# A fused two-layer encoder on one core: normalization moved to ScalarE, page sums made in place, and the starts of three stages rearranged

## The chip, the cores and the metric

The kernel runs on one core of a Trainium2 chip. TensorE (PE) multiplies matrices into eight PSUM banks, VectorE (DVE) and ScalarE (ACT) work on tiles in SBUF and read those banks, GpSimd (POOL) and SyncE (SP) here do little more than start transfers between SBUF and DRAM. Each engine takes its instructions in a fixed order: an instruction that waits holds up all that stand behind it on its engine. The metric is the time of one execution in microseconds (us), lower is better.

## The reference, cut to what matters

An encoder trunk of two layers on x of 1024 positions by 1024 columns, in float32. Layer 0 mixes with attention and a Fourier transform, layer 1 with a spatial gating unit; after each mixer stands a SwiGLU feed-forward network (FFN).

```python
def odd_mixer(x, w_in, norm_g, norm_b, w_s, b_s, w_out):
    z = jax.nn.gelu(x @ w_in, approximate=False)
    u, v = jnp.split(z, 2, axis=-1)                # 2048 columns each
    v = layer_norm(v, norm_g, norm_b)
    vc = v.reshape(B, S // 128, 128, 8, 256)       # chunks, positions, 8 head groups, columns
    s = jnp.einsum('gpq,bnqgc->bnpgc', w_s, vc) + jnp.swapaxes(b_s, 0, 1)[None, None, :, :, None]
    return (u * s.reshape(B, S, 2048)) @ w_out

def swiglu(x, w_gate, w_up, w_down):               # 2816 columns
    return (jax.nn.silu(x @ w_gate) * (x @ w_up)) @ w_down

# each layer
x = layer_norm(DN_ALPHA * x + mixer(x), ...)
x = layer_norm(DN_ALPHA * x + swiglu(x, ...), ...)
```

## The kernel before

**Products.** Every large product is a Strassen-Winograd scheme on a 2 by 2 split: seven products of sums in place of eight. The left operands are sums of the quarters of x (`A11`, `A12`, `A22`, `S1` to `S4`), held transposed for the whole stage; the right operands are sums of the quarters of the weight cells (`t1` to `t4`, `b11`, `b21`, `b22`). A float32 operand is split into a high part, rounded by a cast on ScalarE (L135), and a low part, what is left, by a subtraction on VectorE (L136); `mm3` (L141 to L143) makes high by high, low by high and high by low. One of the seven products of a unit is 12 matmuls of 512 columns. The names tell the side: `xah`/`xal` and `xoh`/`xol` are the halves of left operands, `whi`/`wlo` those of weights, `raw` are loaded weights, `rx` loaded pages, `b` PSUM banks.

**FFN.** `ffn` goes over 22 units of columns. A unit's weights come from `right_operands` (L587), which makes four pairs of tiles `whi`/`wlo`, t4 and t1 in the second of its casts. Those of the first two units are made while the stage before still runs. `seven` (L610) is a generator; each `go(u, 1)` issues one product. The late half of x comes out of the layer norm just before: `turn0` (L490) turns a tile of 128 positions through PSUM by 8 transposes on TensorE, scales and shifts it by 8 instructions on ScalarE (`turned`, L357 to L365), and splits it into `A11` and `A12`; `all_sums` then makes `S2` to `S4`. The first products of units 0 and 1 (t4, t1, on the half that is already there) are issued between the four turns. `v_pair` (L845) does the same at the start of the odd layer, with the columns of v.

**Spatial loop.** After v (written to DRAM as `vd`), a loop over the 8 head groups g (L818) makes u: unit g is seven products, and among them stand four jobs `mixed(n)` of the group before. A job loads its 512 columns of v (`load`), takes mean and deviation off them in four instructions on VectorE (`normed`, L799, for the next job), multiplies them by the position matrix `w_s` into a bank (L808, 8 matmuls of 128 columns), adds the biases (L809, VectorE), and multiplies the page of u in place (L811). `emit` (L823) combines the banks into the page on VectorE (L825) and applies Gelu on ScalarE (L826). A finished page is stored (`tp`, held as `st["H"]`); every two pages `direct` (L343) makes their sums (`page_sums`, L316 to L319, VectorE) into two fresh `raw` tiles and stores them as `SA` and `SB`. The loads of the coming weights use the same four `raw` buffers.

**Output product.** `reduce` loads stored pages, sums and the sums of the output weights (`TA`, `TB`) and multiplies them. The last four jobs (28 to 31) of the loop run among its first products.

A tile's buffer is reused in turn, and who takes it waits for its last reader. `issue_after` and `behind` hold an instruction's place in the order behind another one; a scheduler settles the rest of the order of each engine from the code.

## Time and profile before

| | |
|---|---|
| median of 3 runs | 2571.9 us (2570.29 to 2572.54) |
| profiled execution | 2572.24 us, of which the span from the first to the last instruction is 2570.4 us |
| TensorE busy | 2471.8 us |
| VectorE, ScalarE, GpSimd busy | 1840.0, 1073.5, 308.4 us |
| mean granted clock of TensorE | 0.981 |

The span is what the trace shows; some 2 us of each execution lie around it. The granted clock is the share of TensorE's full speed (2.4 GHz) that it was given, and its two levels are 1.0 and 0.5. A busy TensorE at half clock counts as busy, so the two have to be read together.

### The profile page before, as it was taken

The page shows a single profiled execution, that of the slowest core. Times are in us where ns is not written, and L with a number is a line of the kernel's source. Part 1 is how long each engine was busy: PE and PEld are TensorE (multiplying, and loading weights), DVE is VectorE, ACT ScalarE, POOL GpSimd, SP SyncE. Part 2 cuts the span into 40 slices and gives each one's busy share as a digit, 9 for nine tenths or more (in the row PEclk, how much of TensorE's full clock was granted, in tenths as well). Part 3 has the DMA queues.
Part 4 walks back from the last instruction along what each step waited for, and adds up shares of the span by engine and source line. Part 5 has one row for each costly group of instructions (what it writes and reads, how often), then busy time and mean ns, then how long its engine had stood idle before and what let it go on. Part 6 is the DMA issues. An engine that isn't in the chain of part 4 may idle for free. (4 is left out here: it accounts for less than half of the span.)

```text
span 2570.4 us, 33123 instructions
## 1 busy us (share of the span) xinstructions
PE 2471.8 (96%) x12294; PEld 2083.3 (81%) x12294; DVE 1840.0 (72%) x2673; ACT 1073.5 (42%) x1643; POOL 308.4 (12%) x511
## 2 busy tenths in 40 slices
PE   8989999999999999999999999898999999999997
PEld 6778888887778888878889997776878888887886
DVE  4448878757886667668677767788788766766757
ACT  3335545544653333334355442232474333333332
POOL 1000111010110111110011223221010101101001
PEclk9999999999999999999999999899999999999999
DMA  4122433147334454486645644457634544549554
GB/s 173 42 88 70 143 110 112 62 162 265 127 139 139 173 188 150 161 300 233 205 164 189 214 160 148 147 205 270 228 121 148 175 153 165 188 143 332 198 187 147
DMA packets 164073, 431.95 MB, mean 168 GB/s; under 512 B 19880, under 2 KB 26696, under 8 KB 163912
## 3 DMA queue, kind: packets, MB, share of 16 engines
q1 hardware_dynamic: 108216, 232.11, 27.5%
q0 software_dynamic: 55696, 197.73, 20.6%
q8 instruction: 96, 1.57, 0.3%
q14 instruction: 65, 0.53, 0.1%
HBM read 286.64 MB, written 138.41 MB: 165 GB/s over the span
## 5 line engine op out<-in xcount | busy, mean ns | idle before, releaser
L141 PE MATMUL b<-xoh,whi 128*128 128x512 f32 x1040 | 411.5, 396 | 20.3 <-ACT whi L135 18.4
L136 DVE TENSOR_TENSOR wlo<-raw,whi 128x1024 fp32r<-128x1024 f32 (+3 forms) x277 | 302.7, 1099 | 173.5 <-ACT whi L135 171.0
L135 ACT CAST whi<-raw 128x1024 fp32r<-128x1024 f32 (+3 forms) x277 | 260.6, 953 | 385.3 <-PE b L142 223.6
L135 ACT CAST xoh<-rx 128x1024 fp32r<-128x1024 f32 (+1 forms) x252 | 244.3, 1011 | 421.1 <-PE b L142 323.4
L143 PE MATMUL b<-xoh,wlo 128*128 128x512 f32 x1040 | 408.2, 393 | 0.3
L142 PE MATMUL b<-xol,whi 128*128 128x512 f32 x1040 | 408.3, 393 | 0.0
L136 DVE TENSOR_TENSOR xol<-rx,xoh 128x1024 fp32r<-128x1024 f32 (+1 forms) x252 | 287.3, 1168 | 166.1 <-ACT xoh L135 165.6
L142 PE MATMUL b<-xol,xoh 128*128 128x512 f32 x960 | 380.0, 396 | 17.7 <-DVE xol L136 17.7
L141 PE MATMUL b<-xoh 128*128 128x512 f32 x960 | 377.9, 396 | 14.5 <-ACT xoh L135 14.5
L143 PE MATMUL b<-xoh,xol 128*128 128x512 f32 x960 | 376.9, 393 | 0.0
L141 PEld LDWEIGHTS b<-xoh,whi 128*128 128x128 f32 x1040 | 197.7, 190 | 62.5 <-ACT whi L135 19.4
L143 PEld LDWEIGHTS b<-xoh,wlo 128*128 128x128 f32 x1040 | 197.1, 190 | 44.0 <-DVE wlo L136 3.1
L142 PEld LDWEIGHTS b<-xol,xoh 128*128 128x128 f32 x960 | 183.4, 191 | 59.1 <-DVE xol L136 21.0
L142 PEld LDWEIGHTS b<-xol,whi 128*128 128x128 f32 x1040 | 197.7, 190 | 41.0 <-issue 0.2
L141 PEld LDWEIGHTS b<-xoh 128*128 128x128 f32 x960 | 183.9, 192 | 54.2 <-ACT xoh L135 15.8
L143 PEld LDWEIGHTS b<-xoh,xol 128*128 128x128 f32 x960 | 183.0, 191 | 38.1
L624 ACT COPY y<-b 128x512 f32<-128x512 f32 x200 | 116.6, 587 | 214.2 <-PE b L143 210.1
L141 PE MATMUL b<-xah,whi 128*128 128x512 f32 x416 | 164.9, 396 | 0.1
L142 PE MATMUL b<-xal,whi 128*128 128x512 f32 x416 | 164.0, 394 | 0.0
L143 PE MATMUL b<-xah,wlo 128*128 128x512 f32 x416 | 162.4, 391 | 0.0
L131 DVE TENSOR_TENSOR raw<-raw,raw 128x512 f32<-128x512 f32 (+1 forms) x172 | 127.2, 739 | 24.0 <-DMA raw<-w_up 18.8
L669 DVE TENSOR_TENSOR y<-b,y 128x512 f32<-128x512 f32 x84 | 58.0, 690 | 81.4 <-PE b L143 81.4
(377 smaller groups left out, 4582.8 us busy)
## 6 DMA issues: line engine op xcount, KB each, us to landing
raw<-w_gate SPq DMA_DIRECT2D x44, 512.0 KB, 3.6
raw<-w_up SPq DMA_DIRECT2D x44, 512.0 KB
q<-w_down POOLq DMA_DIRECT2D x44, 512.0 KB, 5.2
h<-x POOLq DMA_DIRECT2D x44, 512.0 KB, 3.8
rx<-h SPq DMA_DIRECT2D x60, 256.0 KB, 3.1
rx<-w_down SPq DMA_DIRECT2D x60, 256.0 KB, 4.9
raw<-o_v SPq DMA_DIRECT2D x16, 512.0 KB, 5.2
x<-o_out POOLq DMA_DIRECT2D x16, 512.0 KB, 6.2
```

Source lines behind the costliest of these rows:

```text
L131: self.nc.vector.tensor_tensor(out, a, b, op=ALU.subtract)
L135: a = self.nc.scalar.copy(hi, src)
L136: return a.ins, self.nc.vector.tensor_tensor(lo, src, hi.bitcast(F32), op=ALU.subtract).ins
L141: mm(ps, lh, rh, start=start, stop=False, skip_group_check=skip)
L142: mm(ps, lh, rl, start=False, stop=False, skip_group_check=skip)
L143: mm(ps, ll, rh, start=False, stop=stop, skip_group_check=skip)
L624: nc.scalar.copy(t, ps)
L669: self.last_v = nc.vector.tensor_tensor(sb, ps, sb, op=op).ins
```

## The change

1. **Second unit of the FFN.** `early_operands`, a generator, takes the place of `right_operands` for unit 1 of each FFN. Its first step makes only t4 and t1, into the first free pair of tiles, ahead of the stage; the second step (b11 with b21, t2 with t3, b22) is taken after `sums`.
2. **Late tiles by twos.** `turned_two` turns two tiles together: the 16 transposes write banks of 2 by 256 columns, and 8 instructions of 256 columns on ScalarE take the place of 16 of 128. The splits take 1024 columns. The same for v (`pend` in `v_pair`).
3. **Normalization on ScalarE.** `normed` is an ACTIVATE with scale 1/deviation and bias `shift` = -mean/deviation, and is placed behind the last Gelu (`last_a`).
4. **Page sums in place.** The sums of the pages of group g are made by `summed(g)` in the pages themselves, two units later (after product 0 of unit g+2), and stored from there; no `raw` tiles are taken.
5. **Pages stored by halves.** Each job stores its 512 columns: 32 stores of 256 KB in place of 16 of 512 KB.
6. **End of the loop.** Job 28 moves into unit 7; jobs 29 to 31 and the sums of groups 6 and 7 run in the output product.

```diff
-                    w0[l].append(self.right_operands(*gate_up(l)(1)))
+                    rest = self.early_operands(*gate_up(l)(1))
+                    w0[l].append((next(rest), rest))
+    def turned_two(self, zs, tiles, gT, bT):
+        ws = [t.rearrange("p (k c) -> p k c", k=4) for t in tiles]
+        pss = [self.bank(i, (P, 2, 256)) for i in range(4)]
+        for k in range(8):
+            for i, z in enumerate(zs):
+                nc.tensor.transpose(pss[k // 2][:, k % 2, i * P:(i + 1) * P], z[:, k * P:(k + 1) * P], self.ident)
+        for k in range(8):
+            nc.scalar.activation(ws[k // 4][:, k % 4, :], pss[k // 2][:, k % 2, :], AF.Identity, bias=bT[:, k:k + 1], scale=gT[:, k:k + 1])
+    def early_operands(self, w1, w2):
+        self.sub(v[:, hi], u[:, lo], g[:, lo])
+        self.sub(v[:, lo], u[:, hi], v[:, hi])
+        self.sub(v[:, lo], v[:, lo], g[:, hi])
+        cells(v, "t4", "t1")
+        yield out
+        cells(g, "b11", "b21")
+        self.sub(v[:, lo], u[:, hi], v[:, hi])
+        self.sub(v[:, hi], u[:, hi], u[:, lo])
+        cells(v, "t2", "t3")
+        cells(u[:, hi], "b22")
...
-                with self.tc.issue_after(self.last_v):
+                with self.tc.issue_after(self.last_a):
-                        nc.vector.tensor_scalar(vz, vz, mv[:, t, 0:1], rstd[:, t:t + 1], op0=ALU.subtract, op1=ALU.mult)
+                        nc.scalar.activation(vz, vz, AF.Identity, bias=shift[:, t:t + 1], scale=rstd[:, t:t + 1])
...
-                if half == 1:
-                    nc.gpsimd.dma_start(st["H"][j], pg[j])
-                    if jj == 1:
-                        self.direct(st, g, pg.pop(j - 1), pg.pop(j), self.raw_tile)
+                nc.gpsimd.dma_start(st["H"][j][:, c], pg[j][:, c])
+            def summed(g, *marks):
+                with self.behind(*marks):
+                    self.page_sums(p0, p1, p0, p1)
+                nc.gpsimd.dma_start(st["SA"][g], p0)
+                nc.gpsimd.dma_start(st["SB"][g], p1)
...
+                    if g > 1 and i == 0:
+                        summed(g - 2, self.last_v)
+                    if g == 7 and i == 6:
+                        mixed(28)
-            return [lambda n=n: mixed(n) for n in range(28, 32)]
+            return [lambda: mixed(29), lambda: (summed(6, self.marks[2]), mixed(30)), lambda: mixed(31), lambda: summed(7, self.marks[2])]
```

**How the order moves.** First, ScalarE at the start of the first FFN. Before: `raw997` to `raw999` are unit 1's weights; whi1002 is its b11 and b21, whi1000 its t4 and t1, and `q1089` is the third late tile.

```order
L135 CAST whi1002_5996<-raw997_5989 128x1024
L365 ACTIVATE q1089_6687<-b1090_6688,bT951_5615,gT950_5614 128x128
L624 COPY y1085_6662<-b1084_6649 128x512
L365 ACTIVATE q1089_6687<-b1090_6688,bT951_5615,gT950_5614 128x128 x3
L365 ACTIVATE q1089_6687<-b1091_6689,bT951_5615,gT950_5614 128x128 x4
L135 CAST xah1079_6624<-q1089_6687 128x4x128
L135 CAST whi1000_5994<-raw999_5993 128x1024
L135 CAST xah1079_6624<-q1089_6687 128x4x128
L624 COPY y1085_6662<-b1092_6710 128x512
L365 ACTIVATE q1093_6724<-b1094_6725,bT951_5615,gT950_5614 128x128 x4
```

Now, at the same place (`q1084` is the first half of the third and fourth tile together; whi1093 is unit 1's b11 and b21):

```order
L135 CAST xah1073_6611<-x1075_6613 128x1024
L135 CAST xah1073_6611<-x1076_6614 128x1024
L135 CAST whi1093_6775<-raw997_5989 128x1024
L378 ACTIVATE q1084_6676<-b1086_6678,bT951_5615,gT950_5614 128x256 x2
L378 ACTIVATE q1084_6676<-b1087_6679,bT951_5615,gT950_5614 128x256
L663 COPY y1082_6660<-b1081_6647 128x512
L663 COPY y1082_6660<-b1083_6662 128x512
L378 ACTIVATE q1084_6676<-b1087_6679,bT951_5615,gT950_5614 128x256
L378 ACTIVATE q1085_6677<-b1088_6680,bT951_5615,gT950_5614 128x256 x2
L378 ACTIVATE q1085_6677<-b1089_6681,bT951_5615,gT950_5614 128x256 x2
L135 CAST xah1073_6611<-q1084_6676 128x1024
```

The cast of t4 and t1 is gone from between the late tiles. It stands some 40 rows further up ScalarE's order, among the casts of the pages `rx` of the product before:

```order
L135 CAST xoh_5606<-rx1010_6101 128x1024
L135 CAST xoh_5606<-rx1011_6106 128x1024
L135 CAST whi1000_5997<-raw999_5993 128x1024
L135 CAST xoh_5606<-rx1012_6135 128x1024
L135 CAST xoh_5606<-rx1013_6140 128x1024
```

Second, VectorE in the spatial loop, at the border of two units. Before, with the sums of the finished pages x1864 and x1865 between a job and the next `normed`:

```order
L799 TENSOR_SCALAR whi1828_13322<-whi1828_13322,vmv1824_13316,vrs1825_13317 128x128 x4
L809 SCALAR_TENSOR_TENSOR wlo1829_13323<-b1900_13838,og1826_13318,q1831_13325 128x512
L811 TENSOR_TENSOR x1865_13516<-x1865_13516,wlo1829_13323 128x512
L316 TENSOR_TENSOR raw1902_13849<-x1864_13515,x1865_13516 128x512
L317 TENSOR_TENSOR raw1901_13848<-x1864_13515 128x512
L318 TENSOR_TENSOR raw1901_13848<-raw1902_13849,x1864_13515 128x512
L825 TENSOR_TENSOR x1889_13706<-b1896_13764,y1892_13721 128x512
L319 TENSOR_TENSOR raw1902_13849<-x1865_13516,raw1901_13848 128x512
L825 TENSOR_TENSOR x1890_13707<-b1896_13764,y1892_13721 128x512
L799 TENSOR_SCALAR whi1828_13322<-whi1828_13322,vmv1824_13316,vrs1825_13317 128x128 x4
L809 SCALAR_TENSOR_TENSOR whi1828_13322<-b1918_13918,og1826_13318,q1831_13325 128x512
```

Now, at the same border some units later (line numbers are shifted: L317 to L320 are the sums, L849 and L851 a job's biases and its product with the page):

```order
L136 TENSOR_TENSOR wlo1957_14228<-raw1947_14216,whi1956_14227 128x512
L317 TENSOR_TENSOR x1911_13848<-x1910_13847,x1911_13848 128x512
L849 SCALAR_TENSOR_TENSOR whi1828_13276<-b1962_14262,og1826_13271,q1831_13279 128x512
L318 TENSOR_TENSOR x1910_13847<-x1910_13847 128x512
L851 TENSOR_TENSOR x1933_14038<-x1933_14038,whi1828_13276 128x512
L319 TENSOR_TENSOR x1910_13847<-x1911_13848,x1910_13847 128x512
L131 TENSOR_TENSOR raw1972_14411<-raw1971_14409,raw1970_14407 128x512
L320 TENSOR_TENSOR x1911_13848<-x1911_13848,x1910_13847 128x512
L849 SCALAR_TENSOR_TENSOR whi1828_13276<-b1964_14296,og1826_13271,q1831_13279 128x512
L136 TENSOR_TENSOR wlo1976_14415<-raw1970_14407,whi1975_14414 128x1024
L851 TENSOR_TENSOR x1933_14038<-x1933_14038,whi1828_13276 128x512
```

The `normed` rows are gone from VectorE, and the sums are those of the group before the last, written into the pages x1910 and x1911 themselves. On ScalarE the `normed` rows (L839) now stand behind Gelu (L872), with casts of weights and copies of banks between them:

```order
L872 ACTIVATE x1865_13472<-x1865_13472 128x512
L839 ACTIVATE whi1828_13276<-whi1828_13276,vshift_13273,vrs1825_13270 128x128 x4
L135 CAST whi1885_13642<-raw1876_13631 128x512
L872 ACTIVATE x1864_13471<-x1864_13471 128x512
L872 ACTIVATE x1865_13472<-x1865_13472 128x512
L839 ACTIVATE whi1828_13276<-whi1828_13276,vshift_13273,vrs1825_13270 128x128 x2
L663 COPY y1890_13671<-b1889_13658 128x512
L839 ACTIVATE whi1828_13276<-whi1828_13276,vshift_13273,vrs1825_13270 128x128 x2
L839 ACTIVATE wlo1829_13277<-wlo1829_13277,vshift_13273,vrs1825_13270 128x128 x4
L135 CAST whi1904_13829<-raw1899_13822 128x1024
```

Third, VectorE at the end of the loop, where the output product's first page operands (`xol` from `rx`) are made. Before:

```order
L136 TENSOR_TENSOR xol_5607<-rx2053_14921,xoh_5606 128x1024
L136 TENSOR_TENSOR xol_5607<-rx2054_14926,xoh_5606 128x1024
L825 TENSOR_TENSOR x2017_14674<-b2021_14703,y2025_14757 128x512
L799 TENSOR_SCALAR whi1828_13322<-whi1828_13322,vmv1824_13316,vrs1825_13317 128x128 x4
L809 SCALAR_TENSOR_TENSOR wlo1829_13323<-b2033_14819,og1826_13318,q1831_13325 128x512
L136 TENSOR_TENSOR xol_5607<-rx2055_14931,xoh_5606 128x1024
L811 TENSOR_TENSOR x1992_14483<-x1992_14483,wlo1829_13323 128x512
L825 TENSOR_TENSOR x2016_14673<-b2023_14731,y2019_14688 128x512
L316 TENSOR_TENSOR raw2035_14830<-x1991_14482,x1992_14483 128x512
L317 TENSOR_TENSOR raw2034_14829<-x1991_14482 128x512
L318 TENSOR_TENSOR raw2034_14829<-raw2035_14830,x1991_14482 128x512
L825 TENSOR_TENSOR x2017_14674<-b2023_14731,y2019_14688 128x512
```

Now (`gb` rows, L469 and L470, are the residual of the layer norm; x2005 is the last page, whose sums begin in the last row):

```order
L320 TENSOR_TENSOR x1982_14433<-x1982_14433,x1981_14432 128x512
L851 TENSOR_TENSOR x2005_14624<-x2005_14624,wlo1829_13277 128x512
L136 TENSOR_TENSOR xol_5607<-rx2047_14984,xoh_5606 128x1024
L849 SCALAR_TENSOR_TENSOR wlo1829_13277<-b2046_14930,og1826_13271,q1831_13279 128x512
L136 TENSOR_TENSOR xol_5607<-rx2048_14989,xoh_5606 128x1024
L851 TENSOR_TENSOR x2005_14624<-x2005_14624,wlo1829_13277 128x512
L469 TENSOR_TENSOR y2033_14831<-y2033_14831,gb2044_14910 128x1024
L136 TENSOR_TENSOR xol_5607<-rx2049_15026,xoh_5606 128x1024
L469 TENSOR_TENSOR q2031_14829<-q2031_14829,gb2044_14910 128x1024
L470 TENSOR_TENSOR y2033_14831<-y2033_14831,gb2045_14912 128x1024
L317 TENSOR_TENSOR x2005_14624<-x2004_14623,x2005_14624 128x512
```

and, five rows later, the end of those sums, four additions of finished banks (L457), and the next page operand:

```order
L320 TENSOR_TENSOR x2005_14624<-x2005_14624,x2004_14623 128x512
L457 SCALAR_TENSOR_TENSOR x2030_14828<-x2030_14828,b2034_14832 128x512
L457 SCALAR_TENSOR_TENSOR q2031_14829<-q2031_14829,b2035_14839 128x512
L457 SCALAR_TENSOR_TENSOR q2032_14830<-q2032_14830,b2037_14858 128x512
L457 SCALAR_TENSOR_TENSOR y2033_14831<-y2033_14831,b2038_14865 128x512
L136 TENSOR_TENSOR xol_5607<-rx2050_15031,xoh_5606 128x1024
```

Before, the sums went into `raw` tiles and stood behind no store; now the sums of the last two groups are in VectorE's order between the operands of the output product, and the operand from rx2050 stands behind them.

## Rows read from the trace of the kernel before

**Rows 1.** Page, part 1, TensorE: busy time, share of the span, instructions.

```profile
PE 2471.8 (96%) x12294; PEld 2083.3 (81%) x12294; DVE 1840.0 (72%) x2673; ACT 1073.5 (42%) x1643; POOL 308.4 (12%) x511
```

**Rows 2.** The waits of TensorE over the whole span: in total, times, longest.

```profile
PE b L141 <- ACT whi L135: 18.4, 5, 6.0
...
PE b L141 <- ACT xoh L135: 14.5, 3, 7.0
PE b L808 <- issue: 7.7, 3, 2.8
```

**Rows 3.** Windows: length, each engine's busy time, granted clock, DMA share, GB/s.

```profile
690.00:742.00 52.00, 46.00 (x208) 37.28 (x208) 44.28 (x71) 36.90 (x73) 6.91 (x11) 0.93 0.25 86
1905.00:1960.00 55.00, 48.19 (x219) 38.97 (x218) 48.36 (x76) 39.11 (x76) 6.27 (x10) 0.97 0.29 101
1360.00:1405.00 45.00, 40.57 (x309) 39.72 (x309) 40.64 (x67) 26.38 (x44) 11.23 (x21) 0.92 0.61 211
1550.00:1715.00 165.00, 147.37 (x692) 121.98 (x691) 125.23 (x245) 46.61 (x68) 45.93 (x70) 0.93 0.43 152
1715.00:1790.00 75.00, 64.81 (x279) 52.71 (x279) 65.69 (x88) 24.93 (x30) 12.96 (x22) 0.91 0.84 289
```

**Rows 4.** Timeline of TensorE, first FFN start: start, length, idle before, releaser.

```profile
707.12 0.80 PE L141 MATMUL b<-xoh,whi 128*128 128x512 f32 x1 [5.00 <-ACT whi L135]
...
727.13 0.50 PE L141 MATMUL b<-xoh,whi 128*128 128x512 f32 x1 [0.97 <-ACT q L624]
```

**Rows 5.** Timeline of ScalarE at the same place.

```profile
697.76 2.59 ACT L365 ACTIVATE x<-b,bT,gT 128x128 f32<-128x128 f32 x7
...
701.18 1.14 ACT L135 CAST whi<-raw 128x1024 fp32r<-128x1024 f32 x1
...
705.87 1.20 ACT L135 CAST whi<-raw 128x1024 fp32r<-128x1024 f32 x1
```

**Rows 6.** Timeline of VectorE at the same place.

```profile
704.35 1.42 DVE L131 TENSOR_TENSOR raw<-raw,raw 128x512 f32<-128x512 f32 x2
```

**Rows 7.** Timeline of VectorE and then TensorE, start of the odd layer's v.

```profile
1363.18 1.29 DVE L136 TENSOR_TENSOR xal<-q,xah 128x512 fp32r<-128x512 f32 x2 [3.51 <-ACT xah L135]
...
1393.74 0.35 PE L862 MATMUL b<-whi,xah 128*128 128x256 f32 x1 [2.15 <-DVE y L873]
```

**Rows 8.** Timeline of TensorE, spatial loop: a product between two stretches, a wait.

```profile
1645.71 0.39 PE L141 MATMUL b<-xah,whi 128*128 128x512 f32 x1
...
1648.43 1.05 PE L808 MATMUL b<-q,whi 128*128 128x128 f32 x8
...
1591.80 0.46 PE L808 MATMUL b<-q,whi 128*128 128x128 f32 x2 [2.76 <-issue]
```

**Rows 9.** Timeline of VectorE ahead of that wait.

```profile
1587.74 0.69 DVE L316 TENSOR_TENSOR raw<-x,x 128x512 f32<-128x512 f32 x1
...
1591.36 0.85 DVE L799 TENSOR_SCALAR whi<-whi,vmv,vrs 128x128 f32<-128x128 f32 x3
```

**Rows 10.** Groups by line and form in 1550 to 1715 us, VectorE and ScalarE.

```profile
L799 DVE TENSOR_SCALAR wlo<-wlo,vmv,vrs 128x128 f32<-128x128 f32 x48 | 14.8, 349 | 0.0
L799 DVE TENSOR_SCALAR whi<-whi,vmv,vrs 128x128 f32<-128x128 f32 x48 | 13.3, 343 | 0.0
...
L809 DVE SCALAR_TENSOR_TENSOR wlo<-b,og,q 128x512 f32<-128x512 f32 x13 | 9.7, 747 | 0.0
...
L826 ACT ACTIVATE x<-x 128x512 f32<-128x512 f32 x24 | 15.2, 632 | 51.1 <-DVE x L825 51.1
```

**Rows 11.** DMA issues in 1550 to 1715 us, then 1715 to 1790 us.

```profile
tp<-x POOLq DMA_DIRECT2D x12, 512.0 KB, 3.5
...
oddSA<-raw POOLq DMA_DIRECT2D x6, 512.0 KB, 4.1
...
tp<-x POOLq DMA_DIRECT2D x4, 512.0 KB, 8.3
```

**Rows 12.** Timeline of ScalarE at the start of the odd layer's output product.

```profile
1756.92 2.95 ACT L135 CAST xoh<-rx 128x1024 fp32r<-128x1024 f32 x3 [10.41 <-DMA rx<-tp]
```

More of the change, by code (lines that the diff above doesn't have):

```diff
@@ L366, in turned @@
         return w[:, 0:4, :], w[:, 4:8, :]
+    def turned_two(self, zs, tiles, gT, bT):
+        nc = self.nc
+        ws = [t.rearrange("p (k c) -> p k c", k=4) for t in tiles]
[5 more added lines that the diff above has]
+            nc.scalar.activation(ws[k // 4][:, k % 4, :], pss[k // 2][:, k % 2, :], AF.Identity, bias=bT[:, k:k + 1], scale=gT[:, k:k + 1])
+        return ws
     def source(self, st, p, m):
@@ L488, in turn1, with turn0 @@
             kept[1, s] = l, h
-        def turn0(s):
-            l, h = self.turned(xt[0, s], (0, 1) if s % 2 == 0 else (2, 3), self.m_tile("xxqq"[s]), gT, bT)
-            self.split(*self.operand(self.A11, s), l)
-            self.late = self.split(*self.operand(self.A12, s), h)[1]
-            kept[0, s] = l, h
+        def turn0(q):
+            ws = self.turned_two([xt[0, 2 * q + i] for i in range(2)], [self.m_tile("xq"[q]) for _ in range(2)], gT, bT)
+            for o, w in zip((self.A11, self.A12), ws):
+                self.late = self.split(*(x[:, q] for x in self.left(o)), w)[1]
+            for i in range(2):
+                kept[0, 2 * q + i] = tuple(w[:, :, i * P:(i + 1) * P] for w in ws)
         def sums(s):
@@ L579, in all_sums @@
                     sums(s)
-        return [lambda s=s: turn0(s) for s in slots], all_sums
+        return [lambda q=q: turn0(q) for q in range(2)], all_sums
     def bcast(self, t, src):
@@ L608, in right_operands, with cells @@
         return out
+    def early_operands(self, w1, w2):
+        g, u = self.raw(w1), self.raw(w2)
+        v = self.raw_tile()
+        lo, hi = self.LO, self.HI
+        out = {}
+        def cells(src, *names):
+            h, l = self.wpair()
+            w = 512 * len(names)
+            self.split(h[:, :w], l[:, :w], src)
+            for i, n in enumerate(names):
+                out[n] = tuple(x[:, i * 512:(i + 1) * 512].rearrange("p (k c) -> p k c", k=4) for x in (h, l))
+        self.sub(v[:, hi], u[:, lo], g[:, lo])
[8 more added lines that the diff above has]
+        cells(u[:, hi], "b22")
+        yield
     def seven(self, w, banks, tiles, emit):
@@ L687, in ffn @@
         w0, w1 = w0
-        u0 = unit(0, w0, "yq")
+        w1, rest = w1
+        u0, u1 = unit(0, w0, "yq"), unit(1, w1, "yq")
         turns[0]()
-        self.go(u0, 1)
+        self.go(u0, 2)
         turns[1]()
-        turns[2]()
-        self.go(u0, 1)
-        turns[3]()
-        u1 = unit(1, w1, "yq")
         self.go(u1, 2)
         sums()
+        next(rest)
         self.go(u0, 5)
@@ L755, in spatial @@
             mv, rstd, ogT, obT = (self.m_tile(n, s, 1) for n, s in (("vmv", (P, NT, 2)), ("vrs", (P, NT)), ("og", (P, 16)), ("ob", (P, 16))))
+            shift = self.small.tile([P, NT], F32, tag="ms", name="vshift")
             for t, n in ((ogT, "o_gT"), (obT, "o_bT")):
@@ L766, in stats @@
                 self.rstd_of(rstd, mv[:, :, 1], LN_EPS)
+                nc.vector.tensor_tensor(shift, mv[:, :, 0], rstd, op=ALU.mult)
+                nc.vector.tensor_scalar(shift, shift, -1.0, None, op0=ALU.mult)
             def biases(i):
@@ L812, in mixed @@
                 load(n + 4)
-                if half == 1:
-                    nc.gpsimd.dma_start(st["H"][j], pg[j])
-                    if jj == 1:
-                        self.direct(st, g, pg.pop(j - 1), pg.pop(j), self.raw_tile)
+                c = slice(half * 512, (half + 1) * 512)
+                nc.gpsimd.dma_start(st["H"][j][:, c], pg[j][:, c])
+            def summed(g, *marks):
+                p0, p1 = pg.pop(2 * g), pg.pop(2 * g + 1)
+                with self.behind(*marks):
+                    self.page_sums(p0, p1, p0, p1)
+                nc.gpsimd.dma_start(st["SA"][g], p0)
+                nc.gpsimd.dma_start(st["SB"][g], p1)
             for g in range(8):
@@ L825, in emit @@
                     self.last_v = nc.vector.tensor_tensor(u, ps, sb, op=op).ins
-                    nc.scalar.activation(u, u, AF.Gelu)
+                    self.last_a = nc.scalar.activation(u, u, AF.Gelu).ins
                 unit = self.seven(w, [(4, 5, 6, 7, 0, 1)[(g * 4 + i) % 6] for i in range(4)], "yy", emit)
@@ L886, in v_pair @@
             for b in range(2):
-                if pend is not None and (n, b) in ((4, 0), (4, 1), (5, 0), (5, 1)):
-                    pend[0][(n - 4) * 2 + b]()
+                if pend is not None and b == 0 and n in (4, 5):
+                    pend[0][n - 4]()
                 if n == 4:
```

## The prediction

> **What bounds the kernel now.** The page comes first: TensorE is busy for 2471.8 of 2570.4 us [rows 1], so the time is its matmuls, the gaps between them, and what it loses at half clock. The view of its waits says who ends the gaps: weights that ScalarE has yet to cast (18.4 us in five waits), page operands that it has yet to cast (14.5 in three), and jobs of the spatial loop (7.7 in three) [rows 2]. Third, the windows of the five stages that the change touches [rows 3]. I read each as: loss = (length - TensorE busy) + (1 - granted clock) x length, the second term for matmuls that took longer at half clock (it counts idle time at half clock too, so it errs upward).
>
> - FFN of layer 0, 690 to 742: 6.0 + 3.6 = 9.6 us.
> - FFN of layer 1, 1905 to 1960: 6.8 + 1.7 = 8.5.
> - Start of v, 1360 to 1405: 4.4 + 3.6 = 8.0.
> - Spatial loop, 1550 to 1715: 17.6 + 11.6 = 29.2.
> - Output product, 1715 to 1790: 10.2 + 6.7 = 16.9.
>
> Together 72 us: no edit here removes a matmul of a product, so that is the most that the change can give. In none of the five is VectorE or ScalarE busy throughout [rows 3]. What counts is where they are late.
>
> **FFN starts.** TensorE sits idle for 5.00 us until the cast of unit 1's weights [rows 4]. ScalarE casts one pair at 701.18, VectorE then makes two more differences at 704.35, and only at 705.87 comes the cast of t4 and t1 [rows 5, 6]. The change makes this pair in the stage before, where its cast and differences (some 1 us and 3 x 0.7 us) stand beside the output product's own work. So the wait goes. What is late next are the sums S2 to S4: the last wait of this start, 0.97 us at 727.13, is for them and what stands around them [rows 4]. They need all four turns. A turn's 8 instructions take 2.59/7 = 0.37 us each [rows 5], 32 of them 11.8 us. An instruction of 256 columns is not in the trace; below it lies 0.37, above it 0.63 (an ACTIVATE of 512 [rows 10]); nearer the lower end I take 0.44, so 16 x 0.44 = 7.0 us, 4.8 saved on ScalarE. That brings the sums some 4 us forward, while TensorE, without its wait, would be there some 8 us earlier: it waits again, about 3 us plus the half clock behind it. Of 9.6 us lost some 6 stay: **3.5 us gained**, bounds 0 and 7. The second FFN has the same waits in the same order (loss 8.5): **3.5 us**, the same bounds.
>
> **Start of v.** VectorE waits 3.51 us for ScalarE's casts of the last turn [rows 7] and then works nearly without a break; some 30 us later TensorE waits for that backlog, 2.15 us at the longest [rows 7]. Turning by twos saves the same 4.8 us on ScalarE, of which some 3 reach the first sum, since transposes and products stand between. A backlog that starts 3 us earlier takes most of 4.4 us of idle time and part of the clock's 3.6: **4.5 us**, bounds 0 and 7.
>
> **Spatial loop.** A product takes 1648.43 - 1645.71 = 2.72 us [rows 8], so a unit of seven with four jobs (8 matmuls of a quarter width, an estimate of 0.45 us) 20.8 us; the window holds (165 - 29.2)/20.8 = 6.5 units, and loses 4.5 us in each. The row that shows how: the page sums begin at 1587.74 on VectorE, `normed` stands behind them and comes only at 1591.36 [rows 9], and TensorE's job waits 2.76 us for it [rows 8]. The longest wait, 6.0 us for a weight cast [rows 2], comes from `raw` tiles that the sums hold until their stores land (4.1 us each [rows 11]), while the coming weights need the same buffers.
>
> Removed from VectorE: 96 `normed`, 14.8 + 13.3 = 28.1 us [rows 10], so 125.2 - 28.1 = 97.1 us, 14.9 a unit. Added to ScalarE: 96 instructions of 128 columns with a scale and a bias per partition, as in a turn: 0.37 each [rows 5], though a turn reads PSUM and these SBUF; the upper bound is again 0.63 [rows 10]. That is 35.5 us (at most 60.5) on 46.6, so 12.6 us a unit (at most 16.5) of 20.8. Neither engine is full. The order shows each `normed` a whole job ahead, and the sums take no `raw` tile. The shift costs two small instructions, once. New is a wait: sums in place need the half store of the last job landed. That job's two VectorE steps (0.75 [rows 10] and about 0.7) and the landing (at most 3.5, as for whole pages [rows 11]) make 5 us; VectorE comes there two products, 5.4 us, later at the earliest, and with its own backlog on the job's side I allow 0 to 3 us of waiting, within the 5.9 that it has free. Behind it wait the next job's steps and weight splits, which are needed products later. So nearly all of the 29.2 goes: **28 us**, bounds 16 (rival 1) and 29.
>
> The Trainium skill speaks against this edit: "ScalarE: Activation LUTs", in its rules for kernel authors, puts adds and multiplies on VectorE, not ScalarE. The same page (What ACT_TABLE_LOAD costs) gives an ACTIVATE with both operands per partition about 280 + 93 + 0.833 ns per column, with 93 ns of overlap, so for 128 columns an estimate of 0.39 us, as the row's 0.37; by it ScalarE would hold 12.9 us a unit. ScalarE is slower here per instruction, as the rule says, than VectorE's 0.29 (28.1/96); but the trace decides by who has time left.
>
> **Output product.** The loss begins with ScalarE waiting 10.41 us for a page that was stored too late [rows 12]; TensorE's share of it is 7.0 us [rows 2]. With job 28 one stage earlier and the first half of a page stored before the second, that store lands earlier, and the wait goes. But the page sums of the last two groups now stand in VectorE's order among the product's operands. A page store lands in 8.3 us here [rows 11], against 3.5 in the loop, and the operand from rx2050 stands behind the last page's sums. By the order and these durations (estimates) TensorE has products until some 24 us after the loop's end; the last half store, issued some 17 us after it, lands at 25, the sums and four bank additions take 5 more: a new wait of up to 7 us, with half clock behind it. Of 16.9 I take **5 us** as gained, bounds -2 and 12.
>
> **Sum.** 3.5 + 3.5 + 4.5 + 28 + 5 = 44.5 us off 2572.2 (the profiled execution's own time, 0.3 above the median) is 2527.7; against the median, 2527.4: **2527 us**. With all terms at their lower bounds 14 us go, at their upper 62.
>
> **The rivals.**
> 1. *Stores hold VectorE.* The sums in place wait not 0 to 3 us but for stores that land as late as in the output product: 4.8 us more, 7.8 in all, 1.9 beyond what VectorE has free; in six units 11 us, twice that with the half clock behind each wait. For it: every job now issues a store and loads through one POOL queue. Against: the loop's transfers take 0.43 of the DMA engines, the output product's 0.84 [rows 3]. 2538 to 2550 us. (The Trainium skill, "DMA: Bandwidth & Descriptors", Anatomy of one DMA, says that most of a fixed 2 us is the receipt of the last byte, so half a store is not half as late; no row here shows a half store.)
> 2. *The starts only move their waits.* The sums in both FFNs and in v set the end, and the early pair gives nothing: 11.5 us less, 2539.
> 3. *Slower: jobs wait for ScalarE.* A `normed` stands behind Gelu, casts and copies in ScalarE's order; if each of the 28 jobs waited 2.4 us (a Gelu of 0.63, four `normed` of 0.37 and the clock's share), 67 us would come on top: 2594. It decides from 44.5/28 = 1.6 us a job. Against it: each `normed` is ordered a product or more ahead, and ScalarE is at 60% of a unit.
> 4. *All 72 us but the clock's last bits go*: about 2505.
>
> **How the numbers follow.** Forecast 0.60, its own range 2514 to 2537 (starts and output product at either end); rival 1 0.17, rival 2 0.12, rival 4 0.05, rival 3 0.04; 0.02 for no change. Range 2510 to 2550: it takes in rivals 1 and 2 and leaves out 3, 4 and the tails. About 0.2% is what a measurement of this kernel can tell from no change. Faster 0.93, same 0.03, slower 0.04.
>
> **What would show it.** Right: in the FFN starts no wait for a weight cast, one of 2 to 4 us ahead of t2; in the loop no wait of TensorE over 1 us, 20.8 to 21.5 us a unit, granted clock near 1.0; VectorE's idle time there ends at tp stores for at most 3 us a unit. Wrong: TensorE waiting for L839 (rival 3), VectorE waiting over 6 us for tp stores with TensorE behind it (rival 1), the loop's weight casts still late, or a wait of over 10 us in the output product for operands behind the sums.

## The result, and the profile after

The changed kernel takes 2540.3 us (median of 4 runs, 2537.2 to 2541.8) against 2572.2 us; the ratio is 0.9878, 95% interval 0.9864 to 0.9891. So it is 31.9 us faster, where 44.5 were forecast. The time lies within the range of 2510 to 2550, above the forecast's own (2514 to 2537), and where rivals 1 and 2 had put it; whether it came there by their ways is another matter.

Page, part 1, of the changed kernel, which answers to [rows 1]:

```profile
span 2540.0 us, 33155 instructions
...
PE 2456.4 (97%) x12294; PEld 2073.4 (82%) x12294; DVE 1808.9 (71%) x2537; ACT 1111.1 (44%) x1711; POOL 318.5 (13%) x527
```

Its three largest waits of TensorE by sum (line, what it waited for: us in total, times, longest), to set against [rows 2] (L848 is L808 of before, L839 is `normed`), and below them a wait of the kernel before that [rows 2] leaves out:

```profile
PE b L142 <- DVE xol L136: 22.3, 8, 6.6
PE b L141 <- ACT xoh L135: 16.4, 4, 5.0
PE b L848 <- ACT whi L839: 8.9, 1, 8.9
```

```profile
PE b L142 <- DVE xol L136: 17.7, 8, 5.4
```

The waits of L141 for weight casts are gone, and so are the jobs' of [rows 2]. Page operands were waited for before too, 17.7 and 14.5 us; now it is 22.3 and 16.4, the second including the sums of the FFN starts. New is one wait of 8.9 us for a normalization on ScalarE. The five windows, same lengths and stages as [rows 3] (later stages begin earlier now; columns as there: length, busy time of PE, PEld, DVE, ACT, POOL, granted clock, DMA share, GB/s):

```profile
690.00:742.00 52.00, 48.26 (x215) 39.02 (x215) 42.16 (x65) 32.44 (x53) 7.38 (x12) 0.93 0.27 94
...
1355.00:1400.00 45.00, 43.86 (x361) 43.25 (x360) 40.91 (x66) 26.32 (x43) 11.23 (x21) 1.00 0.64 218
...
1690.00:1765.00 75.00, 59.52 (x264) 49.19 (x263) 61.94 (x70) 29.76 (x41) 10.06 (x18) 0.89 0.79 280
1525.00:1690.00 165.00, 165.00 (x834) 139.65 (x833) 117.39 (x172) 100.50 (x197) 61.10 (x94) 1.00 0.53 172
1867.00:1922.00 55.00, 48.35 (x214) 38.54 (x213) 43.84 (x68) 32.59 (x53) 6.34 (x10) 0.94 0.24 87
```

Read as the prediction read them, (length - busy) + (1 - clock) x length:

| stage | lost before | lost after | gained | forecast | gained, idle time counted once |
|---|---|---|---|---|---|
| FFN of layer 0 | 9.6 | 3.7 + 3.6 = 7.4 | 2.2 | 3.5 | 1.5 |
| FFN of layer 1 | 8.5 | 6.7 + 3.3 = 10.0 | -1.5 | 3.5 | -1.1 |
| start of v | 8.0 | 1.1 + 0 = 1.1 | 6.9 | 4.5 | 6.3 |
| spatial loop | 29.2 | 0 | 29.2 | 28 | 27.6 |
| output product | 16.9 | 15.5 + 8.3 = 23.7 | -6.8 | 5 | -2.6 |
| sum | 72.2 | 42.2 | 30.0 | 44.5 | 31.7 |

The last column is needed because the formula counts idle time at half clock twice, which the prediction mentions. Windows of the changed kernel cut to stretches with a granted clock of 0.50, one in the first FFN and two at the output product's waits:

```profile
721.40:728.20 6.80, 6.06 (x14) 4.41 (x15) 6.76 (x11) 4.21 (x6) 0.00 (x0) 0.50 0.26 80
1694.20:1704.40 10.20, 3.24 (x12) 2.96 (x13) 6.26 (x8) 7.34 (x14) 2.55 (x4) 0.50 1.04 398
1731.80:1738.50 6.70, 2.92 (x7) 2.34 (x8) 6.70 (x9) 0.00 (x0) 1.60 (x3) 0.50 0.84 294
```

The formula takes half of each stretch as lost, but in the output product TensorE is busy for only 6.2 of these 16.9 us. Matmuls of 512 columns start 0.43 us apart there, against 0.23 at full clock, so about half of the busy time is lost. Idle time plus that half gives 16.0 us lost before and 18.6 after in the output product, and the last column in all.

The traces also allow a check without any formula, since both have 12294 matmuls in nearly the same order (numbered from 0 here). From the 7800th to the 9000th, which takes in the loop's jobs and the output product, they took 285.5 us and now take 258.3: 27.2 less. The first FFN's start (3600th to 3850th) gained 1.6 us and the start of v (6700th to 6900th) 6.3; the second FFN's (9450th to 9700th) lost 1.3. From the 12150th to the end 3.5 us are lost, for a reason that no run here looks into.

The two spans differ by 2570.4 - 2540.0 = 30.4 us. In the loop TensorE is busy for all of 165 us at full clock; the forecast for that is right, and it is nearly the whole result. What is missing against 44.5 is missing, by the last column, in the output product (7.6), in the second FFN (4.6) and in the first (2.0); v gave 1.8 more, and the rest lies outside the five windows.

**The output product's first wait**, timelines of ScalarE, VectorE and TensorE of the changed kernel (start, length, instruction, idle before and what ended it):

```profile
1692.64 1.04 ACT L135 CAST xoh<-rx 128x1024 fp32r<-128x1024 f32 x1 [6.36 <-DMA rx<-tp]
1695.19 1.04 ACT L135 CAST xoh<-rx 128x1024 fp32r<-128x1024 f32 x1 [1.50 <-DMA rx<-o_out]
1697.82 1.04 ACT L135 CAST xoh<-rx 128x1024 fp32r<-128x1024 f32 x1 [1.59 <-DMA rx<-tp]
1699.14 1.04 ACT L135 CAST xoh<-rx 128x1024 fp32r<-128x1024 f32 x1 [0.28 <-DMA rx<-o_out]
1700.10 0.62 ACT L872 ACTIVATE x<-x 128x512 f32<-128x512 f32 x1
1700.63 1.63 ACT L839 ACTIVATE whi<-whi,vshift,vrs 128x128 f32<-128x128 f32 x4
...
1693.72 1.23 DVE L136 TENSOR_TENSOR xol<-rx,xoh 128x1024 fp32r<-128x1024 f32 x1 [8.19 <-ACT xoh L135]
...
1697.40 0.69 DVE L871 TENSOR_TENSOR x<-b,y 128x512 f32<-128x512 f32 x1
...
1701.16 0.79 PE L848 MATMUL b<-q,whi 128*128 128x128 f32 x2 [8.93 <-ACT whi L839]
```

Read it from the bottom: job 28 waits 8.93 us for its normalization, which stands on ScalarE behind a Gelu (1700.10). The Gelu's input comes late, at 1697.40 on VectorE (L871), behind splits of page operands that wait for their casts. By the time it is there, ScalarE has two more casts ahead of the Gelu in its order (1697.82 and 1699.14). The four casts wait 6.36, 1.50, 1.59 and 0.28 us for what they read to be loaded. None of these steps takes long; each stands in order behind one that waits for a transfer. **The second wait**, same views:

```profile
1726.10 0.69 DVE L317 TENSOR_TENSOR x<-x,x 128x512 f32<-128x512 f32 x1 [1.93 <-DMA tp<-x]
1726.70 1.22 DVE L470 TENSOR_TENSOR q<-q,gb 128x1024 f32<-128x1024 f32 x1
...
1731.31 0.69 DVE L320 TENSOR_TENSOR x<-x,x 128x512 f32<-128x512 f32 x1
...
1734.30 5.77 DVE L136 TENSOR_TENSOR xol<-rx,xoh 128x1024 fp32r<-128x1024 f32 x5
...
1735.58 0.79 PE L142 MATMUL b<-xol,xoh 128*128 128x512 f32 x1 [6.55 <-DVE xol L136]
```

The last page's sums begin at 1726.10, when the half store has landed, and end at 1732.0, with three additions of the residual (L469 and L470, the first at 1726.70) between the four; four additions of banks follow, and only then the operand that TensorE has waited 6.55 us for. This one was forecast, with up to 7 us.

**The FFN starts.** TensorE's timeline in the first FFN, and its waits in the second (1867 to 1923 us):

```profile
722.14 1.89 PE L141 MATMUL b<-xoh,whi 128*128 128x512 f32 x3 [3.74 <-ACT xoh L135]
```

```profile
PE b L141 <- ACT xoh L135: 4.2, 1, 4.2
PE b L141 <- ACT xah L135: 1.3, 2, 1.1
PE b L376 <- DVE q L484: 1.2, 1, 1.2
```

No weight cast any more. The same matmul, number 3770, starts at 722.14 in place of 727.13 [rows 4], but after 3.74 us of idle time at once, and at half clock. In the second FFN the products wait 1.3 us for a cast of 1024 columns, which they did not before; the transposes' wait (1.2) is hardly new, it was 0.9 before.

**The half stores.** VectorE's wait for them in the loop, and their landing times (first line of its tile view that gives them):

```profile
DVE x L317 <- DMA tp<-x: 23.2, 6, 5.6
```

```profile
DMA to landing us min/median/max: 2.8/3.5/5.7
```

Six waits, 3.9 us on average, 5.6 at the longest: more than the 0 to 3 forecast, within the 5.9 us that the prediction left VectorE, and TensorE never waits. A half store lands in 3.5 us, as a whole page did [rows 11].

### The profile page after: what moved, and what is told of

Its sections match the earlier page's. It is cut to its first block, busy times and chain, and to the rows that moved or that the text cites. A ratio compares the mean times of both kernels' runs of the same rounds, so it can differ in the third digit from the quotient of the medians.

```text
span 2540.0 us, 33155 instructions
## 1 busy us (share of the span) xinstructions
PE 2456.4 (97%) x12294; PEld 2073.4 (82%) x12294; DVE 1808.9 (71%) x2537; ACT 1111.1 (44%) x1711; POOL 318.5 (13%) x527
## 3 DMA queue, kind: packets, MB, share of 16 engines
q0 software_dynamic: 55952, 197.73, 20.9%
## 4 chain that ended last, share of the span: by engine, by line
PE 81%; DVE 6%; issue 5%; DMA 4%; ACT 2%; POOL 1%; SPq 1%; DVEq 0%; ACTq 0%; POOLq 0%
PE b L142 18%; PE b L141 18%; PE b L143 18%; PE S L1316 6%; PE b L912 5%; PE mm L141 4%; PE mm L142 4%; PE mm L143 4%; PE mm L1335 2%; DVE xol L136 1%; DMA rx<-h 1%; PE b L848 1%; DMA x<-xs 1%; ACT xoh L135 1%; DVE st L475 1%
## 5 line engine op out<-in xcount | busy, mean ns | idle before, releaser
L141 PE MATMUL b<-xoh,whi 128*128 128x512 f32 x1040 | 410.7, 396 | 7.9 <-ACT xoh L135 7.9
L142 PE MATMUL b<-xol,xoh 128*128 128x512 f32 x960 | 379.4, 395 | 22.3 <-DVE xol L136 22.3
L141 PE MATMUL b<-xoh 128*128 128x512 f32 x960 | 376.1, 394 | 8.5 <-ACT xoh L135 8.5
L141 PEld LDWEIGHTS b<-xoh,whi 128*128 128x128 f32 x1040 | 196.6, 189 | 50.3 <-ACT xoh L135 8.8
L141 PEld LDWEIGHTS b<-xoh 128*128 128x128 f32 x960 | 182.9, 190 | 47.6 <-ACT xoh L135 9.3
L141 PE MATMUL b<-xah,whi 128*128 128x512 f32 x416 | 162.5, 391 | 1.3 <-ACT xah L135 1.3
```

What stands on the lines that cost most here:

```text
L141: mm(ps, lh, rh, start=start, stop=False, skip_group_check=skip)
L142: mm(ps, lh, rl, start=False, stop=False, skip_group_check=skip)
```

## The experiments

Each kernel was timed with the kernel before on the same chip; where medians of different groups are compared, the ratio is the better measure. "Stage loss" is the idle time of TensorE plus half of the time that it was busy at half clock, for the output product in the window 1685 to 1765.

**1 and 2. The parts apart.** One kernel with only the loop's part (items 3 to 6), one with only the starts (items 1 and 2).

> Only the loop's part of the change (normalization on ScalarE, sums in place, halves, job 28 in unit 7); both FFN starts and the start of v as before. Theory (the starts gave some 6.5 us, the loop some 31, and the end of the loop took 5 back): 2572 - 26 = 2546 us. Rival (each start gave its forecast, 11.5 us together, and the loop only the rest): 2551 us.

> Only the three starts (second unit's operands in two steps, late tiles by twos); loop and output product as before. Theory: the start of v gives 6 us, the first FFN 1.6, the second loses 1.4, so 2572 - 6.5 = 2565.5 us. Rival: the forecast's 11.5 us, 2560.5.

Measured: 2550.3 us against 2571.4, ratio 0.9918 (0.9900 to 0.9937), and 2564.0, 0.9973 (0.9961 to 0.9985): 21 and 7.5 us, 28.7 together for 31.9 of the whole. The parts add up, within their intervals. That the starts would give 11.5 us (the second rival) is refuted; the loop's part came out at the first rival's number, 4 us above its theory, whose 2546 lies at the edge of its interval.

**3. Normalization back on VectorE**, the rest of the change kept.

```diff
-                with self.tc.issue_after(self.last_a):
+                with self.tc.issue_after(self.last_v):
-                        nc.scalar.activation(vz, vz, AF.Identity, bias=shift[:, t:t + 1], scale=rstd[:, t:t + 1])
+                        nc.vector.tensor_scalar(vz, vz, mv[:, t, 0:1], rstd[:, t:t + 1], op0=ALU.subtract, op1=ALU.mult)
```

> The changed kernel with the normalization back on VectorE, behind the last bank combination, all else as changed. Theory: VectorE then holds 14.9 + 4.5 us of work a unit and the 3 to 4 us that it waits for half stores, over the 20.8 of a unit, so it becomes the bound of the loop: 2 us a unit and half clock behind it, 2552 to 2560 us. Rival: the loop's gain came from the weight tiles that the sums set free, and normalization was hidden anyway: 2540, or less, since job 28 then waits for no cast on ScalarE.

Measured: 2541.9 us, ratio 0.9891 (0.9876 to 0.9907); the changed kernel's is 0.9878. The theory fell: moving the normalization, the edit that I had worked out at greatest length, is worth nothing that can be measured. Windows of the loop and of the output product, and below them the latter of the changed kernel:

```profile
1535.00:1690.00 155.00, 152.50 (x765) 127.89 (x764) 132.00 (x262) 52.61 (x78) 57.40 (x89) 1.00 0.51 168
...
1685.00:1765.00 80.00, 66.95 (x298) 54.12 (x298) 72.13 (x99) 24.04 (x26) 15.80 (x27) 0.96 0.83 290
```

```profile
1685.00:1765.00 80.00, 64.52 (x290) 53.47 (x290) 62.47 (x71) 30.36 (x43) 12.59 (x22) 0.89 0.80 279
```

VectorE is busy for 132.0 of 155 us in the loop (111.5 in the changed kernel), and TensorE still loses only 2.5. In the output product the stage loss is 13.1 + 3.4 = 16.5 us, against 15.5 + 3.1 = 18.6: there the place behind ScalarE's casts costs about what the loop gains.

**4. Page sums into raw tiles again**, at once, as before; the rest kept.

```diff
                 nc.gpsimd.dma_start(st["H"][j][:, c], pg[j][:, c])
+                if half == 1 and jj == 1:
+                    self.direct(st, g, pg.pop(j - 1), pg.pop(j), self.raw_tile)
...
-                    if g > 1 and i == 0:
-                        summed(g - 2, self.last_v)
```

> The changed kernel with the page sums into raw tiles again, at once after the second page's last job, all else as changed. Theory: weights wait again for the stores of the sums (before: 6.3 + 3.3 us at one place, some 4 elsewhere), but VectorE has time; and the last group's sums no longer hold the output product (8 us): 2540 + 10 - 8 = 2542 us. Rival: the gain was all VectorE's: 2540 - 8 = 2532.

Measured: 2564.5 us, ratio 0.9976 (0.9966 to 0.9987). Neither: 24 us of the gain are lost. The loop's window, waits of SyncE's queue and of VectorE there, and one of TensorE's waits with what leads to it:

```profile
1535.00:1690.00 155.00, 139.78 (x666) 116.67 (x665) 94.98 (x136) 81.09 (x162) 51.50 (x79) 0.94 0.44 150
```

```profile
SPq L158 <- DMA oddSA<-raw: 44.4, 2, 25.7
SPq L396 <- DMA oddSB<-raw: 19.6, 1, 19.6
SPq L811 <- DMA oddSA<-raw: 17.3, 1, 17.3
```

```profile
DVE raw L131 <- DMA oddSA<-raw: 5.6, 5, 1.4
```

```profile
1645.39 0.69 DVE L131 TENSOR_TENSOR raw<-raw,raw 128x512 f32<-128x512 f32 x1 [1.60 <-DMA raw<-o_u]
...
1648.88 2.51 ACT L135 CAST whi<-raw 128x1024 fp32r<-128x1024 f32 x3 [6.66 <-DVE raw L131]
...
1649.98 0.79 PE L141 MATMUL b<-xoh,whi 128*128 128x512 f32 x1 [4.53 <-ACT whi L135]
```

The loop's window loses 15.2 + 7.4 = 22.6 us again. No job waits there now, and 14.9 of the 15.2 idle us end with a weight cast; before, in 1550 to 1715, jobs ended 9.0 us and weight casts 8.5. SyncE's queue, which loads the weights in order, stands for 44 + 20 + 17 us behind stores of sums that hold the raw tiles, and in the changed kernel for 0.5 (there it waits for readers of the weights). So a weight comes late: VectorE waits 1.60 us for it at 1645.39, ScalarE 6.66 us for its differences, and TensorE 4.53 us for the cast. That is the longest of the waits. Ahead of others VectorE itself waits for a store of sums to leave the tile that it writes differences into (5.6 us in five waits).

**5. Page sums in place alone**, on the kernel before: normalization on VectorE, whole pages, job 28 and starts as before.

> The kernel before with one part of the change alone: page sums in place, two units later; normalization on VectorE, whole pages stored, job 28 and all starts as before. Theory: what held the loop were the raw tiles that the sums kept until their stores landed, so this part alone gives most of the loop's gain: 2570 - 25 = 2545 us, as the kernel with the loop's whole change (2550). Rival: VectorE's load was what counted, the sums in place only add waits to it: 2565 to 2575.

Measured: 2551.5 us, ratio 0.9925 (0.9909 to 0.9942), the same as the loop's whole part (0.9918). Its loop loses 4.4 us at full clock:

```profile
1535.00:1690.00 155.00, 150.57 (x751) 125.45 (x751) 129.52 (x257) 53.03 (x79) 46.97 (x70) 1.00 0.47 154
```

Experiments 4 and 5 agree: the loop's gain comes from the sums being in place and two units later (which were not tried apart), and without that the raw tiles hold the weights. With `normed` on VectorE, TensorE waits for jobs for only 2.7 us in this window. Normalization, half stores and job 28 together add nothing that the times show. In the profiled executions the 7800th to the 9000th matmul take 20.3 us less than before with the sums alone and 25.2 with the loop's whole part, so up to 5 us may be theirs; two kernels with the same loop differ by 2 us in that stretch.

**6 to 8. The output product's two waits.** Job 28 back among its matmuls; the last group's sums behind the next pass's first product; both.

```diff
-                    if g == 7 and i == 6:
-                        mixed(28)
-            return [lambda: mixed(29), lambda: (summed(6, self.marks[2]), mixed(30)), lambda: mixed(31), lambda: summed(7, self.marks[2])]
+            self.rest7 = lambda m: summed(7, m)
+            return [lambda: mixed(28), lambda: mixed(29), lambda: (summed(6, self.marks[2]), mixed(30)), lambda: mixed(31)]
...
+                if (p, g) == (5, 0) and self.rest7 is not None:
+                    self.rest7(self.marks[2])
```

> The changed kernel with job 28 back among the output product's first matmuls. Theory: TensorE's 8.9 us wait came from job 28 standing ahead of a product whose operands were there, while its normalization stood behind casts that waited for pages; it goes with its half clock, 9 to 11 us: 2530 us. Rival: the pages arrive late all the same, and the first products wait for them in its place: 2537 to 2540.

> The changed kernel with the last group's page sums placed behind the first product of the next pass of the output product. Theory: the 6.6 us wait for the operand from rx2050 was VectorE standing at the last half store and in those sums: 6.7 + 1.5 go, 2532 us. Rival: VectorE is late with the residual's work anyway, and the wait stays: 2538 to 2540.

> Both: job 28 back and the last sums late. Theory: the two waits are independent, 2540 - 10 - 8 = 2522 us. Rival: what the one gives, the other takes, since an output product that starts sooner meets its pages and sums sooner: 2530.

Measured: 2539.0 (0.9887, 0.9872 to 0.9901), 2541.0 (0.9892, 0.9877 to 0.9907) and 2546.3 us (0.9912, 0.9896 to 0.9929): no gain, and both together rather slower. The first two rivals hold; for both together theory (2522) and rival (2530) were both wrong. Windows of the first two:

```profile
1685.00:1765.00 80.00, 66.67 (x280) 54.46 (x279) 62.59 (x70) 29.94 (x41) 11.17 (x20) 0.87 0.79 279
```

```profile
1685.00:1765.00 80.00, 64.06 (x277) 51.78 (x276) 61.70 (x69) 28.57 (x40) 11.57 (x21) 0.91 0.78 275
```

Stage losses 13.3 + 7.5 = 20.9 and 15.9 + 5.0 = 20.9 us, and 16.5 + 5.0 = 21.5 for both, against 18.6. Job 28 back stands only 6 matmuls further on, and TensorE still waits 6.6 us for its normalization. With the last sums late, the wait for rx2050's operand shrinks from 6.55 us to 2.1, and a later one of 4.3 us, for another operand of VectorE's, takes its place.

**9. The page casts behind job 28's normalization** in the order.

```diff
-            self.marks = (sp, *self.split(h[:, :n], l[:, :n], r[:, :n]))
+            with self.behind(*marks):      # marks: job 28's last ACTIVATE, in the first pass only
+                self.marks = (sp, *self.split(h[:, :n], l[:, :n], r[:, :n]))
```

> The changed kernel with the casts of the output product's next page operands held behind job 28's normalization in the order; nothing else. Theory: ScalarE's casts wait 6.4 us for pages, and behind them stand unit 7's bank combinations, their Gelu and the normalization that TensorE waits 8.9 us for; with the order turned they run in that time, and TensorE comes to the next operands 2 to 4 us before they are there: 6 to 8 us less, 2533 us. Rival (as for job 28 and for the last sums): the output product's operands and VectorE's work there set the end, and a later wait takes what this one gives: 2539 to 2542.

Measured: 2538.4 us, ratio 0.9875 (0.9860 to 0.9890). Again the rival. Its window, and VectorE's waits in the stage:

```profile
1685.00:1765.00 80.00, 67.47 (x294) 54.75 (x293) 63.12 (x72) 30.77 (x44) 13.01 (x23) 0.91 0.84 291
```

```profile
DVE x L317 <- DMA tp<-x: 6.1, 1, 6.1
DVE q L470 <- DMA q<-xs: 3.6, 1, 3.6
```

The chain of the first wait is shown right (it is gone), but VectorE now stands 6.1 us at a half store ahead of group 6's sums and 3.6 us at a residual, with page operands behind both: 12.5 + 4.6 = 17.2 us are lost.

**10. The sums at the starts kind by kind**, on the changed kernel.

```diff
-                for s in slots:
-                    sums(s)                    # S2, S4, S3 of one tile after the other
+                for s in slots:                # the same for S4, then for S3
+                    (a11, a12), (a21, s1) = kept[0, s], kept[1, s]
+                    self.sub(s1, s1, a11)
+                    self.split(*self.operand(self.S2, s), s1)
```

> The changed kernel with the sums at the three starts made kind by kind (all four of S2, then S4, then S3) in place of tile by tile. Theory: after the change the FFN starts wait for the fourth tile's S2 behind the other tiles' S4 and S3, so S2 comes some 6 us sooner and the waits of 3.7 and 4.2 us with their half clock go, 7 us in each FFN: 2526 us. Rival: the sums' whole work on VectorE sets the end, and b22 or t3 wait in t2's place: 2537 to 2541.

Measured: 2530.1 us, ratio 0.9849 (0.9835 to 0.9864), 10 us below the changed kernel by the medians and 7.5 by the ratios. Windows of the three starts:

```profile
690.00:742.00 52.00, 51.22 (x240) 41.82 (x239) 44.30 (x70) 34.15 (x55) 8.45 (x14) 1.00 0.29 102
1865.00:1920.00 55.00, 51.34 (x239) 41.47 (x238) 45.52 (x71) 34.22 (x55) 6.88 (x12) 1.00 0.28 102
1355.00:1400.00 45.00, 43.45 (x363) 43.25 (x362) 43.40 (x69) 25.23 (x38) 11.24 (x21) 1.00 0.61 216
```

They lose 0.8, 3.7 and 1.6 us, at full clock, for 6.8, 9.6 and 1.1.

**11. Kind by kind, without the early operands** (`right_operands` for the second unit, as before).

> The changed kernel with the sums kind by kind, but the FFN's second unit's operands made all at once and late, as before. Theory: early operands and the order of the sums each remove one of two waits that stand one behind the other; with the sums no longer late, the early operands are worth the 5 us waits and their half clock, 7 us in each FFN: 2530 + 14 = 2544 us. Rival: the early operands are worth nothing, here as in the change: 2530.

Measured: 2541.0 us, ratio 0.9886 (0.9871 to 0.9900). Windows of the two FFN starts, and TensorE's wait in the first:

```profile
690.00:742.00 52.00, 47.69 (x214) 38.76 (x213) 45.33 (x70) 33.01 (x54) 7.47 (x12) 0.93 0.25 88
1867.00:1922.00 55.00, 47.77 (x214) 38.55 (x213) 46.93 (x73) 34.89 (x59) 6.78 (x10) 0.94 0.21 78
```

```profile
PE b L141 <- ACT whi L135: 4.3, 1, 4.3
```

The wait for the weight cast is back, 6.9 and 10.0 us are lost. So with the sums in time, the early operands are worth some 10 us (2541.0 - 2530.1 = 10.9, and 9.5 by the ratios). In the change, items 1 and 2 together gave 0.4 us in the two FFN starts, counted once: the sums' wait stood behind the one that they removed. The changed kernel without the early operands alone was not run, so what they gave there by themselves is not shown.

**12. All the orders together.**

> A version meant to beat both: the changed kernel with the sums kind by kind, the page casts behind job 28's normalization, and in the output product the next pass's first operands made before the residual's work, group 6's sums after job 31 and group 7's after the next pass's first product. Theory: kind by kind gives its 10 us here too; in the output product VectorE's order, not its amount of work, makes the 19 us lost, and with the operands ahead of everything that waits for a store some 8 of them go: 2522 us. Rival: the transfers (0.88 of the DMA engines there) or the work itself set the end of that stage, and only the 10 us are left: 2529 to 2531.

Measured: 2532.8 us (2529.7 to 2537.1), ratio 0.9850 (0.9825 to 0.9876): as experiment 10, and near the rival's number. Its interval overlaps the changed kernel's. The output product's window:

```profile
1685.00:1765.00 80.00, 68.68 (x288) 54.86 (x287) 63.45 (x70) 30.46 (x42) 10.07 (x18) 0.91 0.83 299
```

In the profiled execution the stage loses 11.3 + 5.8 = 17.1 us, 1.5 less than in the changed kernel, and the 7800th to the 9000th matmul take 26.5 us less than before, where the changed kernel gained 27.2. So this order gained nothing in that stage that can be told.

## Why the prediction was right or wrong

The total lies in the range partly by luck. The loop came out as forecast in size, but for another reason than the one with the most weight; and the misses at the output product and the FFNs brought the time to where rivals 1 and 2 had it, though rival 1's cause is refuted.

- **Spatial loop, 28 us: right in size (29.2, or 27.6 counted once), wrong in what it laid it to.** The step "Removed from VectorE: 96 `normed`" was given the weight, with the `raw` tiles as the longest wait beside it. Experiments 3 to 5 show the reverse: moving the sums gives most of it, and VectorE has time for the normalization. The mistake is to read a 2.76 us wait behind page sums [rows 8, 9] as VectorE's load: with the sums moved and `normed` still on VectorE (experiment 5), the jobs' 9.0 us of waiting were down to 2.7.
- **A unit of the loop** takes 22.7 us at full clock, not 20.8 to 21.5. A job was taken at 0.45 us, but its 8 matmuls take 0.80 until the next one can start; [rows 8] has 1.05 for them to the end of the last. Nothing in the result hung on it.
- **The waits of TensorE** were read without the second largest, 17.7 us for page operands that VectorE has yet to split; in the output product that kind became the 6.55 us wait.
- **The wait for half stores** is there, and larger than allowed, and hidden, as worked out. Rival 1 is refuted at its bound: no wait in the loop passed 5.9 us.
- **Output product, 5 us: wrong, -6.8 by the formula and -2.6 counted once.** Half of the step held: the wait for the last group's sums came as described (6.55 us for "up to 7"). What failed is "With job 28 one stage earlier ... the wait goes": one wait went, and job 28 met another, 8.9 us, of the kind that rival 3 describes, at the one place where page casts stand ahead of the normalization. I had looked for what stands behind the new wait on VectorE, not for what stands ahead of job 28 on ScalarE.
- **FFN starts, 3.5 us each: mis-sized, 2.2 and -1.5 (1.5 and -1.1 counted once).** That the sums are late next, and by how much (about 3 us; 3.7 and 4.2), was right. The clock behind the new wait was named but not priced: TensorE is busy at half clock for 6.1 and 6.0 us, some 3 us lost in each, against 2.3 and 1.6 before. And the products of the second FFN wait 1.3 us for the larger casts. Rival 2 holds for the FFNs, not for v; experiments 10 and 11 show its mechanism, a wait that stands right behind the one removed.
- **Start of v, 4.5 us: 6.9 (6.3),** since both the idle time and the clock's share went.
- **ScalarE's instruction**: four `normed` take 1.63 us, 0.41 each; 0.37 was taken. From the figures of the Trainium skill, "ScalarE: Activation LUTs" (What ACT_TABLE_LOAD costs), the prediction worked out an estimate of 0.39. The rule of the same page of the Trainium skill against adds and multiplies on this engine (Rules for kernel authors) would have made the kernel neither faster nor slower here: experiment 3.

What stays open is what bounds the output product's start. Six kernels (experiments 6 to 10 and 12, the tenth with the changed kernel's own order there) lose 17.1 to 21.5 us each in the profiled executions, the changed kernel 18.6, experiment 3 16.5 and the kernel before 17.9 (1709 to 1789), while the transfers of the six are at 0.77 to 0.84 and VectorE is busy for 62 to 64 of 80 us. In the stretch around the first wait the DMA engines are busy throughout (1.04 at 398 GB/s in 1694.2 to 1704.4), as they were around the 7.0 us wait of the kernel before (1.00 in 1747 to 1758). That no order tried there made the kernel measurably faster is shown; that transfers are the cause is not, for no run changed how much is transferred there.

## What to carry to other kernels

When a wait is removed, find the next one in the order of each engine, and look whether it is the same length: the early operands and the turns by twos gave 0.4 us in the FFN starts, and with the sums behind them reordered the early operands are worth some 10. A tile that was held until its store landed delayed the loads and differences that share its buffers, and what stood behind them on the loading queue; look at that queue's waits before counting an engine's work. When idle time and half clock are added up, count an idle stretch at half clock once. An instruction moved to an idle engine joins that engine's order: what stands ahead of it there, and waits for transfers, is now ahead of its readers too.

## What the runs showed of the hardware

Halving a store did not halve its landing time. In the loop of experiment 4 stores of 256 KB landed in a median of 2.9 us, with the DMA engines at 0.44; before, those of 512 KB took 3.5, at 0.43 [rows 3, 11].

```profile
tp<-x POOLq DMA_DIRECT2D x23, 256.0 KB, 2.9
```

An idle stretch of 3.74 us of TensorE cost some 3 us more: of the following 6.8 us at a granted clock of 0.50 it was busy for 6.06, in the first FFN. The kind-by-kind kernel kept 1.00 in both FFN starts, with 0.8 us idle in the first and 3.7 in the second, there in pieces of 1.1 us at most.
